# Causal attention: score chunks in pairs of PSUM banks with one exponential per pair, and the low parts of the probabilities multiplied side by side at a block's end

## The chip, the cores and the metric

The kernel runs on one core of a Trainium2 chip. The metric is the device time of one execution in microseconds (us), from the first to the last instruction, as the median of several runs. The engines are TensorE (PE, with its weight load PEld), VectorE (DVE), ScalarE (ACT), GpSimd (POOL) and SyncE (SP). PE writes its results to PSUM, which has eight banks of 512 f32 per partition.

## The reference

The reference is a small decoder trunk: one Mamba-2 layer, then one layer of multi-head latent attention, over 2048 tokens of 1024 channels. The change touches only the attention (16 heads, 96 channels for queries and keys, 64 for values):

```python
def causal_block_attention(q_nope, q_rope, k_nope, k_rope, v):
    scale = (QK_NOPE + QK_ROPE) ** -0.5
    for i in range(S // Q_BLOCK):
        q0 = i * Q_BLOCK
        kv_len = q0 + Q_BLOCK
        s = jnp.einsum('bqhd,bkhd->bhqk', q_nope[:, q0:kv_len], k_nope[:, :kv_len]) + \
            jnp.einsum('bqhr,bkr->bhqk', q_rope[:, q0:kv_len], k_rope[:, :kv_len])
        s = s.astype(jnp.float32) * scale
        mask = (q0 + local)[:, None] >= jnp.arange(kv_len)[None, :]
        p = jax.nn.softmax(jnp.where(mask, s, -jnp.inf), axis=-1).astype(v.dtype)
        outs.append(jnp.einsum('bhqk,bkhd->bqhd', p, v[:, :kv_len]))
```

## The kernel before, in words

The program has three stages, one after the other on PE: the Mamba layer and the projections for queries, keys and values (`layers`), the attention (`attention`, `heads`), and the gate, the output projection and the last norm (`back`). Numbers that need more than one pass of PE's precision are kept as a high and a low part.

**Blocks, rows, chunks.** For each of 16 heads there are four query blocks (0 to 3) of 512 queries. A block has four rows of 128 queries. A row's scores run over all keys up to its diagonal and are cut (`cuts`) into chunks of 256 to 512 keys: one chunk a row in block 0, two in block 1, three in block 2, four in block 3, 40 a head. What follows is per chunk, row or block:

- Scores, per chunk: three products of PE (L85 to L87: high by high, high by low, low by high) into one bank `mm` of PSUM. The row's last chunk also gets the causal mask added by a product (L1046, or L1044 in the first row). The pool gives out four banks `mm` in turn; another four, `tr`, serve transposes and outputs. The first 18 chunks of the stage take `tr` and `mm` in turn.
- Maximum: DVE takes the maximum of each chunk (L1047, `mx`). At a row's end it takes the maximum of those, negated (L1051, `nm`).
- Exponential, per chunk: ACT (L1059) reads the bank, subtracts `nm`, writes the probabilities `Pr` and sums them into `sm`; this frees the bank. DVE adds a row's sums (L1063).
- Transposes, "T", per 128 keys of a block: PE turns the four rows' probabilities (L1074) into one bank `tr`. ACT copies the bank to f16 as the high part (L116), DVE makes the low part from bank and high part (L117); both lie in one tile `PTs`.
- Value products, "V": PE multiplies the 128 columns of the values (64 high, 64 low) with the high part (L1084) and with the low part (L1085), 512 columns of queries or fewer at the diagonal. All go into one bank, the output `O`, whose partitions 0 to 63 and 64 to 127 are added by the store. After the block's last one, ACT copies the bank (L1091) and it is stored.

**Order.** PE's order in this stage is written by hand: `ahead` yields after every chunk, and the table `CREDIT` says for each chunk of a row which T and V follow it, from chunk 20 on (`LAG`). So the score chunks run some 20 chunks ahead of the T and V of their block. A V is taken once more than two T are held (`DEPTH`). The orders of DVE, ACT and POOL come from a scheduler at build time; every engine works through its queue in order. PE's next row can begin when a bank `mm` is free, that is when the exponential of the chunk four places before is done; that exponential needs its row's `nm`, and so the maximum of its row's last chunk.

Of the kernel before, what the change touches and what calls it, by code (L numbers as in the profile page):

```python
# [20 lines left out]
P = 128  # L21
# [47 lines left out]
class Net:  # L69
# [5 lines left out]
    def name(self, s):  # L75
        self.n += 1
        return f"{s}_{self.n}"

    def t(self, pool, tag, shape, dt=F32, bufs=None):
        return pool.tile(shape, dt, name=self.name(tag), tag=tag, bufs=bufs)  # L80


# [227 lines left out]
    def layers(self):  # L310
        with ExitStack() as ctx:
            tc = self.tc
            early = ExitStack()
# [682 lines left out]
    def attention(self):  # L996
        with ExitStack() as ctx:
            self.wo = self.tail.enter_context(self.tc.tile_pool(name="wo", bufs=1, side="right", reuse_waits="tile"))
            self.wraw = []
            sp = ctx.enter_context(self.tc.tile_pool(name="asp", bufs=2, reuse_waits="tile"))  # L1000
            with self.tc.manual_schedule(engines={mybir.EngineType.PE}):
                self.heads(sp)

    def heads(self, sp):
        nc, v = self.nc, self.nc.vector
        begun = []
# [12 lines left out]

        def scores(h, qb, st):  # L1020

            if h + 1 < NH:
                if qb == 2:
                    self.load_k(h + 1, 0, NB)
                    self.load_v(h + 1)
                self.load_q(h + 1, qb)
            Q, K = quer.pop((h, qb)), keys[h]
            late = []
            for j in range(4):
                qs = slice(j * P, (j + 1) * P)  # L1030
# [3 lines left out]
                banks = []  # L1034
                for n, (c0, w) in enumerate(parts):
                    if late:
                        late.pop(0)()
                    begun.append(0)
# [3 lines left out]
                    if n == nb - 1:  # L1042
                        if qb == j == 0:
                            nc.tensor.matmul(s[:, 0:w], self.idb, self.mk, start=False, stop=True)  # L1044
                        else:
                            nc.tensor.matmul(s[:, w - P:w], self.idb, self.mk[:, 0:P], start=False, stop=True)  # L1046
                    v.tensor_reduce(mx[:, n:n + 1], s[:, :w], AX.X, ALU.max)  # L1047
# [3 lines left out]
                v.tensor_reduce(nm, mx[:, :nb], AX.X, ALU.max, negate=True)  # L1051
                p = {}
                sm = self.t(sp, "sm", [P, 4], bufs=4)
                st["P"].append(p)

                def exp(n, j=j, nb=nb, parts=parts, banks=banks, nm=nm, p=p, sm=sm):
                    s, w = banks[n]
                    x = self.t(sp, "Pr", [P, TB], bufs=NP)
                    nc.scalar.activation(x[:, :w], s[:, :w], AF.Exp, bias=nm, accum_out=sm[:, n:n + 1])  # L1059
                    for c in range(0, w, P):  # L1060
                        p[(parts[n][0] + c) // P] = x[:, c:c + P]
                    if n == nb - 1:
                        v.tensor_reduce(sums[h][:, 4 * qb + j:4 * qb + j + 1], sm[:, :nb], AX.X, ALU.add)  # L1063

                late += [lambda n=n, f=exp: f(n) for n in range(nb)]
            for f in late:
                f()

        def turn(h, qb, kb, st):

            jj = max(kb - 4 * qb, 0)
            pt = self.t(self.pp, "tr", [P, TB], bufs=4)
            for j in range(jj, 4):
                nc.tensor.transpose(pt[:, j * P:(j + 1) * P], st["P"][j][kb], self.ident)  # L1074
# [3 lines left out]
            return u[:, :, c], c  # L1078

        def values(h, qb, kb, st, u, c):  # L1080
            if kb == 0:
                st["O"] = self.t(self.pp, "tr", [P, TB], bufs=4)
            nk = 4 * qb + 4
            nc.tensor.matmul(st["O"][:, c], vals[h][:, kb, :], u[:, 0], start=kb == 0, stop=False)  # L1084
            nc.tensor.matmul(st["O"][:, c], vals[h][:, kb, :], u[:, 1], start=False, stop=kb == nk - 1)  # L1085
            if kb == nk - 1:
                finish(h, qb, st)

        def finish(h, qb, st):
            o = self.t(sp, "Os", [P, TB], bufs=3)  # L1090
# [18 lines left out]
        states = [{"P": []} for _ in jobs]  # L1109
        sums = {}  # L1110
        def ahead():
            for n, (h, qb) in enumerate(jobs):
# [5 lines left out]
        held = []  # L1118

        def work(what):  # L1120

# [2 lines left out]
                held.append((a, turn(*a)))  # L1124
            elif what == "V" and held and (len(held) > DEPTH or not units):
                a, (u, c) = held.pop(0)
                values(*a, u, c)

        step = 0
        for credit in ahead():  # L1130
            step += 1
            if step > LAG:
                for what in credit:
                    work(what)
        while units or held:
            work("T")
            work("V")


    def back(self):  # L1140
        nc, a, v, hp = self.nc, self.a, self.nc.vector, self.hp
        with ExitStack() as ctx:
            sp = ctx.enter_context(self.tc.tile_pool(name="bsp", bufs=2, reuse_waits="tile"))
            self.sp = sp
            us = self.t(self.sm, "us", [P, KD])
            nc.sync.dma_start(us, self.us_d.rearrange("(k p) -> p k", p=P))
# [186 lines left out]
```

## Time and profile before

| what | value |
|---|---|
| median of 3 runs (lowest to highest) | 3209.99 us (3205.72 to 3210.55) |
| the profiled execution itself, its span | 3210.4 us, 3208.6 us |
| granted TensorE clock, mean | 0.997 |
| attention stage, from its first score product to its end | 2095 to 3027 us of the span |
| time of a head in the middle of that stage | 57 us |
| memory traffic | 322 MB read, 115 MB written, 136 GB/s |

A stretch of the profile gives for each engine its busy time and, in brackets, its instructions. A row of the timeline gives the start and the length in us, the engine, the line, the operation, out<-in by the program's names, and in square brackets the idle time before it and who ended it. A group gives the count, then the busy time in us and the mean length of one in ns. A matmul's length holds the depth of the array's pipeline: its pace is the distance from one start to the next. Lines are those of the kernel before; in the changed one L85 to L87 are L92 to L94, L1074 is L1090, L1084 is L1099, L1085 is L1110, L1059 is L1071 and L1047 is L1059.

### The profile page before, as it was taken

To read this page: it belongs to the slowest core of one execution; us is meant where nothing else is said; L and a number is where in the kernel's file an instruction comes from. 1 tells how busy PE (TensorE), PEld (TensorE's weight loads), DVE (VectorE), ACT (ScalarE), POOL (GpSimd) and SP (SyncE) were. 2 spreads that over 40 slices of the span, in tenths; PEclk is the share of its full clock that TensorE was granted. 3 is DMA by queue.
4 is the path that set the end of the run, shared out by engine and by line. 5 is a ranking of instruction groups with operands and counts; after the bars stand their busy time and mean duration, and the time that the engine had idled before them with its cause. 6 is when DMAs were issued, how large, how long until landed. Compare 5 with 4: busy or idle time off the path is not lost.

```text
span 3208.6 us, 52002 instructions
## 1 busy us (share of the span) xinstructions
PE 3101.7 (97%) x17735; PEld 2245.6 (70%) x17735; DVE 2511.8 (78%) x5330; ACT 2024.2 (63%) x5123; POOL 661.9 (21%) x895
## 2 busy tenths in 40 slices
PE   8999999999999999999999999999999999999998
PEld 6777654555655566555888888877777777777776
DVE  6888898888777787877876665678888888888665
ACT  7878566665555554556656554477877778778522
POOL 1222123322122212321121211322222122122100
PEclk9999999999999999999999999999999999999999
DMA  5333445553343344423376655853444444444485
GB/s 176 99 98 106 136 150 210 166 164 129 102 148 96 101 129 160 136 89 122 114 261 216 223 194 194 261 115 76 91 82 85 84 78 94 80 98 99 113 260 156
DMA packets 208632, 440.61 MB, mean 137 GB/s; under 512 B 28464, under 2 KB 62256, under 8 KB 206928
## 3 DMA queue, kind: packets, MB, share of 16 engines
q1 hardware_dynamic: 160672, 290.86, 29.4%
q0 software_dynamic: 47696, 146.44, 17.8%
q8 instruction: 140, 2.29, 0.3%
q14 instruction: 124, 1.02, 0.1%
HBM read 321.85 MB, written 115.35 MB: 136 GB/s over the span
## 4 chain that ended last, share of the span: by engine, by line
PE 62%; DVE 17%; ACT 7%; DMA 6%; issue 6%; POOL 1%; SPq 1%; ACTq 0%; DVEq 0%; POOLq 0%
PE mm L85 12%; PE mm L87 12%; PE mm L86 12%; PE tr L1074 6%; DVE cacc L488 4%; PE tr L86 3%; PE tr L1084 3%; PE tr L1085 3%; PE tr L85 3%; PE tr L87 3%; DMA wraw<-in_ssm_w_in_dram 2%; DMA big<-cumT 2%; DVE big L661 1%; DVE wsp L112 1%; DMA os<-ri_d 1%
## 5 line engine op out<-in xcount | busy, mean ns | idle before, releaser
L117 DVE SCALAR_TENSOR_TENSOR PTs<-tr,PTs 128x512 f16<-128x512 f32 (+3 forms) x640 | 374.4, 606 | 93.0 <-ACT PTs L116 87.3
L116 ACT ACTIVATE PTs<-tr 128x512 f16<-128x512 f32 (+3 forms) x640 | 328.1, 540 | 140.3 <-PE tr L1074 139.6
L1047 DVE TENSOR_REDUCE mx<-mm 128x1 f32<-128x512 f32 (+2 forms) x631 | 375.0, 606 | 45.4 <-PE mm L87 43.0
L1059 ACT ACTIVATE Pr<-mm,nm 128x512 f32<-128x512 f32 (+2 forms) x631 | 395.1, 635 | 22.9 <-DVE nm L1051 21.4
L1074 PE MATMUL tr<-pack,Pr 128*128 128x128 f32 x2176 | 317.5, 273 | 1.5 <-ACT Os L1091 1.4
L87 PE MATMUL mm<-xT,wsp 128*128 128x512 f16 (+1 forms) x800 | 308.3, 386 | 3.5 <-DVE wsp L117 2.3
L85 PE MATMUL mm<-xT,wsp 128*128 128x512 f16 (+1 forms) x800 | 311.4, 389 | 0.0
L85 PE MATMUL mm<-K,xT 96*128 96x512 f32 (+2 forms) x639 | 286.1, 448 | 23.3 <-ACT Pr L1059 22.1
L86 PE MATMUL mm<-xT,wsp 128*128 128x512 f16 (+1 forms) x800 | 308.1, 385 | 0.0
L1074 PEld LDWEIGHTS tr<-pack,Pr 128*128 128x128 f32 x2176 | 253.2, 141 | 50.0 <-ACT Os L1091 2.2
L675 ACT ACTIVATE Xw<-tr,d_wend 128x64 f32<-128x64 f32 x512 | 182.5, 357 | 93.5 <-DVE Xd L671 85.7
L85 PE MATMUL mm<-wsp,xT 128*128 128x512 f16 (+2 forms) x640 | 235.4, 368 | 4.5 <-ACT craw L482 4.4
L86 PE MATMUL mm<-wsp,xT 128*128 128x512 f16 (+2 forms) x640 | 234.0, 366 | 0.0
L87 PE MATMUL mm<-wsp,xT 128*128 128x512 f16 (+2 forms) x640 | 233.6, 366 | 0.0
L86 PE MATMUL mm<-K,xT 96*128 96x512 f32 (+2 forms) x639 | 231.2, 362 | 0.0
L87 PE MATMUL mm<-K,xT 96*128 96x512 f32 (+2 forms) x639 | 231.0, 361 | 0.0
L488 DVE SCALAR_TENSOR_TENSOR cacc<-craw,pack,cacc 128x512 f32<-128x512 f32 x288 | 217.1, 776 | 10.3 <-ACT cacc L486 9.3
L1084 PE MATMUL tr<-PTs,xT 128*128 128x512 f16 (+3 forms) x640 | 222.0, 348 | 0.1
L1085 PE MATMUL tr<-PTs,xT 128*128 128x512 f16 (+3 forms) x640 | 219.4, 347 | 0.0
L85 PE MATMUL mm<-wsp,yT 128*128 128x512 f32 x512 | 208.5, 408 | 3.3 <-DVE hs L545 2.1
L633 POOL TENSOR_TENSOR Xp<-Xw,Xp 128x512 fp32r<-128x512 f32 x64 | 83.0, 1296 | 607.7 <-ACT Xp L632 395.0
L87 PE MATMUL mm<-wsp,yT 128*128 128x512 f32 x512 | 204.3, 399 | 0.0
(420 smaller groups left out, 7818.9 us busy)
## 6 DMA issues: line engine op xcount, KB each, us to landing
wraw<-in_ssm_w_in_dram SPq DMA_DIRECT2D x128, 256.0 KB, 3.0
big<-cumT SPq DMA_DIRECT2D x64, 512.0 KB, 4.8
wraw<-in_ssm_w_out_dram SPq DMA_DIRECT2D x128, 256.0 KB, 2.7
wsp<-w_d SPq DMA_DIRECT2D x64, 512.0 KB, 3.7
w_d<-wsp POOLq DMA_DIRECT2D x32, 512.0 KB, 4.5
xT<-qn_d POOLq DMA_DIRECT2D x64, 256.0 KB, 4.6
K<-kn_d POOLq DMA_DIRECT2D x15, 1024.0 KB, 8.2
wraw<-in_mla_w_uq_dram SPq DMA_DIRECT2D x36, 256.0 KB, 4.9
```

Source lines behind the costliest of these rows:

```text
L85: mm(out, l_hi, r_hi, start=start, stop=False)
L86: mm(out, l_hi, r_lo, start=False, stop=False)
L87: mm(out, l_lo, r_hi, start=False, stop=stop)
L116: self.nc.scalar.activation(hi, src, AF.Copy, scale=scale)
L117: self.nc.vector.scalar_tensor_tensor(lo, src, scale, hi, ALU.mult, ALU.subtract)
L488: nc.vector.scalar_tensor_tensor(acc, raw[:, k:k + TB], wk[k], acc, ALU.mult, ALU.add)
L675: act(Xw[:, hc], px[:, hc], AF.Copy, scale=wend[:, h0 + h:h0 + h + 1])
L1047: v.tensor_reduce(mx[:, n:n + 1], s[:, :w], AX.X, ALU.max)
L1059: nc.scalar.activation(x[:, :w], s[:, :w], AF.Exp, bias=nm, accum_out=sm[:, n:n + 1])
L1074: nc.tensor.transpose(pt[:, j * P:(j + 1) * P], st["P"][j][kb], self.ident)
L1084: nc.tensor.matmul(st["O"][:, c], vals[h][:, kb, :], u[:, 0], start=kb == 0, stop=False)
L1085: nc.tensor.matmul(st["O"][:, c], vals[h][:, kb, :], u[:, 1], start=False, stop=kb == nk - 1)
```

## The change

- The scores of two neighbouring chunks go to one tile `pair` of two banks; two such tiles take the place of the four banks `mm`. `cuts` gives pairs of equal widths (or a single chunk), so some rows have 2 x 320, 2 x 384 or 2 x 448 in place of 512 and a rest. The count of chunks and of maxima stays. The first 18 chunks no longer use `tr`.
- One exponential serves a pair: 24 a head in place of 40, up to 1024 wide. A row with one exponential (blocks 0 and 1) has its sum copied by POOL in place of added by DVE.
- High and low part of the transposed probabilities are two tiles, 5 and 18 of them. `values` multiplies only the high part. The low parts are kept until the block's last V; then `lows` multiplies them with the 64 high columns of the values alone, the even ones into partitions 0 to 63 of `O`, the odd ones into 64 to 127. The product of the low values with the low probabilities is left out. `lows` runs at the end of the next row of scores, or ahead of the next block's first V. Only then is `O` copied and stored.
- `CREDIT`, `LAG` and `DEPTH` are unchanged.

```diff
-NP = 24
+NP = 14
+NL = 18
...
+        self.pm = ctx.enter_context(self.tc.tile_pool(name="pm", bufs=4, space=PSUM, reuse_waits="tile"))
...
             while at < kv:
-                w = min(TB, kv - at)
-                if kv - at == TB + P:
-                    w = 384
-                out.append((at, max(w, 256)))
+                w = min(2 * TB, kv - at)
+                if kv - at == 2 * TB + P:
+                    w -= P
+                out.append((at, 1, max(w, 256)) if w <= TB else (at, 2, w // 2))
                 at += w
...
-                    s = self.t(self.pp, "tr" if len(begun) <= 18 and len(begun) % 2 == 1 else "mm", [P, TB], bufs=4)
-                    ks = slice(c0, c0 + w)
-                    self.mm3(s[:, :w], Q[:, 0, qs], Q[:, 1, qs], K[:, 0, ks], K[:, 1, ks], True, n < nb - 1)
...
-                    v.tensor_reduce(mx[:, n:n + 1], s[:, :w], AX.X, ALU.max)
-                    banks.append((s, w))
-                    yield CREDIT[qb][j][n]
+                for c0, m, w in parts:
+                    for i in range(m):
+                        if late:
+                            late.pop(0)()
+                        if i == 0:
+                            pair = self.t(self.pm, "pair", [P, 2, TB], bufs=2)
+                            banks.append(pair[:, :m, :w])
+                        s, ks = pair[:, i, :w], slice(c0 + i * w, c0 + i * w + w)
+                        end = n == total - 1
+                        self.mm3(s, Q[:, 0, qs], Q[:, 1, qs], K[:, 0, ks], K[:, 1, ks], True, not end)
...
+                        v.tensor_reduce(mx[:, n:n + 1], s, AX.X, ALU.max)
+                        yield CREDIT[qb][j][n], end
+                        n += 1
...
-                    x = self.t(sp, "Pr", [P, TB], bufs=NP)
-                    nc.scalar.activation(x[:, :w], s[:, :w], AF.Exp, bias=nm, accum_out=sm[:, n:n + 1])
+                    x = self.t(sp, "Pr", [P, 2 * TB], bufs=NP)[:, :m * w]
+                    nc.scalar.activation(x.rearrange("p (m w) -> p m w", m=m), banks[n], AF.Exp, bias=nm,
+                                         accum_out=sm[:, n:n + 1])
...
-            u = self.t(sp, "PTs", [P, 2, TB], F16, bufs=5)
-            self.pair16(u[:, 0, c], u[:, 1, c], pt[:, c], PSCALE)
+            hi, lo = self.t(sp, "PTh", [P, TB], F16, bufs=5), self.t(sp, "PTl", [P, TB], F16, bufs=NL)
+            self.pair16(hi[:, c], lo[:, c], pt[:, c], PSCALE)
...
-            nc.tensor.matmul(st["O"][:, c], vals[h][:, kb, :], u[:, 0], start=kb == 0, stop=False)
-            nc.tensor.matmul(st["O"][:, c], vals[h][:, kb, :], u[:, 1], start=False, stop=kb == nk - 1)
+            nc.tensor.matmul(st["O"][:, c], vals[h][:, kb, :], u[0], start=kb == 0, stop=False)
...
+        def lows(h, qb, st):
+            nk = len(st["lo"])
+            for i, (kb, l, c) in enumerate(st["lo"]):
+                d = slice(i % 2 * 64, i % 2 * 64 + 64)
+                nc.tensor.matmul(st["O"][d, c], vals[h][:, kb, 0:64], l, start=False, stop=i >= nk - 2)
+            finish(h, qb, st)
...
             if step > LAG:
+                if end and owed:
+                    lows(*owed.pop())
```

On PE, the last two chunks of row 1 of block 3 in a middle head stood as follows (`mm` are score banks, K the keys, xT the queries, mk and idb the mask; in brackets the engine whose semaphore a row waits for):

```order
L85 MATMUL mm_24712<-K_23572,xT_23810 128x512 [waits Activation_49]
L86 MATMUL mm_24712<-K_23572,xT_23810 128x512
L87 MATMUL mm_24712<-K_23572,xT_23810 128x512
L85 MATMUL mm_24720<-K_23572,xT_23810 128x256 [waits Activation_49]
L86 MATMUL mm_24720<-K_23572,xT_23810 128x256
L87 MATMUL mm_24720<-K_23572,xT_23810 128x256
```

In the changed program the same two chunks on PE are halves of one tile `pair`:

```order
L92 MATMUL pair_24674<-K_23538,xT_23780 128x384 [waits Activation_49]
L93 MATMUL pair_24674<-K_23538,xT_23780 128x384
L94 MATMUL pair_24674<-K_23538,xT_23780 128x384
L92 MATMUL pair_24674<-K_23538,xT_23780 128x384 [waits DVE_49]
L93 MATMUL pair_24674<-K_23538,xT_23780 128x384
L94 MATMUL pair_24674<-K_23538,xT_23780 128x384
```

The widths became equal, and the second chunk waits for DVE: in the program the awaited count is that of the maximum over the first chunk of the same tile. All 256 pairs with two chunks have this wait.

On ACT, around the change from row 1 to row 2 of that block, before (`PTs` are high copies of transposes, `Pr` exponentials):

```order
L116 ACTIVATE PTs_24698<-tr_24694 128x384 [waits PE_49,Activation_49]
L116 ACTIVATE PTs_24731<-tr_24728 128x256 [waits PE_49,Activation_49]
L116 ACTIVATE PTs_24736<-tr_24734 128x128 [waits PE_49,Activation_49]
L1059 ACTIVATE Pr_24755,sm_24753<-mm_24689,nm_24751 128x512 [waits DVE_49]
L116 ACTIVATE PTs_24746<-tr_24741 128x512 [waits PE_49,Activation_49]
L1059 ACTIVATE Pr_24770,sm_24753<-mm_24703,nm_24751 128x512
```

On ACT, at the same place in the changed program:

```order
L123 ACTIVATE PTh_24662<-tr_24658 128x384 [waits PE_49,Activation_49]
L123 ACTIVATE PTh_24688<-tr_24685 128x256 [waits PE_49,Activation_49]
L123 ACTIVATE PTh_24694<-tr_24692 128x128 [waits DVE_49,PE_49]
L1071 ACTIVATE Pr_24713,sm_24711<-pair_24653,nm_24709 128x1024 [waits DVE_49]
L123 ACTIVATE PTh_24704<-tr_24699 128x512 [waits PE_49,Activation_49]
L1071 ACTIVATE Pr_24729,sm_24711<-pair_24674,nm_24709 128x768
```

The copies keep their places ahead of the first exponential, and that one now reads 1024 columns; the next row's first chunk waits for it.

On PE, where query block 1 (eight units of T and V) ends, the changed program has its low parts in one batch (`tr_24635` is the output, 64 partitions wide in each row):

```order
L1110 MATMUL tr_24635<-PTl_24643,xT_23541 64x512
L1110 LDWEIGHTS xT_23541
L1110 MATMUL tr_24635<-PTl_24663,xT_23541 64x384
L1110 LDWEIGHTS xT_23541
L1110 MATMUL tr_24635<-PTl_24689,xT_23541 64x256
L1110 LDWEIGHTS xT_23541
L1110 MATMUL tr_24635<-PTl_24695,xT_23541 64x128
L1090 MATMUL tr_24760<-pack,Pr_24391 128x128
```

Before, each of these stood right behind its high product (L1084, then L1085, both 128 partitions); now the last four of eight stand in a row behind a row of scores, and the transposes follow.

More of the change, by code (lines that the diff above doesn't have):

```diff
@@ L312, in layers @@
             tc = self.tc
+            self.banks(ctx)
             early = ExitStack()
@@ L999, in attention @@
             self.wraw = []
+            self.banks(ctx)
             sp = ctx.enter_context(self.tc.tile_pool(name="asp", bufs=2, reuse_waits="tile"))
@@ L1033, in scores @@
                 mx = self.t(sp, "mx", [P, 4], bufs=4)
[L1034 to L1038, printed above, removed]
[L1039 to L1049 removed]
+                banks, n = [], 0
+                total = sum(m for _, m, _ in parts)
+                for c0, m, w in parts:
[8 more added lines that the diff above has]
+                        self.mm3(s, Q[:, 0, qs], Q[:, 1, qs], K[:, 0, ks], K[:, 1, ks], True, not end)
+                        if end:
+                            if qb == j == 0:
+                                nc.tensor.matmul(s, self.idb, self.mk, start=False, stop=True)
+                            else:
+                                nc.tensor.matmul(s[:, w - P:w], self.idb, self.mk[:, 0:P], start=False, stop=True)
+                        v.tensor_reduce(mx[:, n:n + 1], s, AX.X, ALU.max)
+                        yield CREDIT[qb][j][n], end
+                        n += 1
                 nm = self.t(sp, "nm", [P, 1], bufs=4)
[L1051 removed]
+                v.tensor_reduce(nm, mx[:, :total], AX.X, ALU.max, negate=True)
                 p = {}
@@ L1126, in work @@
                 a, (u, c) = held.pop(0)
+                if a[2] == 0 and owed:
+                    lows(*owed.pop())
                 values(*a, u, c)
         step = 0
-        for credit in ahead():
+        for credit, end in ahead():
             step += 1
             if step > LAG:
+                if end and owed:
+                    lows(*owed.pop())
                 for what in credit:
@@ L1143, in back @@
             sp = ctx.enter_context(self.tc.tile_pool(name="bsp", bufs=2, reuse_waits="tile"))
+            self.banks(ctx)
             self.sp = sp
```

28 lines of the change are left out of this document (17 added, 11 removed).

## The prediction

> **What bounds the kernel now.** I read the page's engine line first, then the attention stage alone, then its waits, then single rows. The engine line and the chain that ended last say that TensorE (PE) carries the kernel:
>
> ```profile
> span 3208.6 us, 52002 instructions
> PE 3101.7 (97%) x17735; PEld 2245.6 (70%) x17735; DVE 2511.8 (78%) x5330; ACT 2024.2 (63%) x5123; POOL 661.9 (21%) x895
> PE 62%; DVE 17%; ACT 7%; DMA 6%; issue 6%; POOL 1%; SPq 1%; ACTq 0%; DVEq 0%; POOLq 0%
> ```
>
> The change touches the attention, so the stretches of that stage matter (columns: length; busy time of PE, weight load, DVE, ACT, POOL; clock):
>
> ```profile
> 2095.00:3027.00 932.00, 906.26 (x5696) 693.34 (x5694) 773.23 (x1833) 733.83 (x2012) 202.64 (x297) 1.00 0.43 86
> 2227.00:2284.00 57.00, 55.73 (x355) 42.81 (x354) 48.01 (x115) 45.19 (x128) 12.02 (x20) 1.00 0.42 84
> 2455.00:2512.00 57.00, 55.73 (x355) 42.81 (x354) 48.00 (x115) 45.20 (x128) 12.02 (x20) 1.00 0.43 84
> ```
>
> The reader sees a strict period: one head every 57.00 us, sixteen heads in 932 us, PE idle 1.27 us a head. DVE and ACT have 9 and 12 us to spare, so PE's own stream sets the pace, as long as no wait is put into it. The waits of that stage show how little PE stands still:
>
> ```profile
> DVE mx L1047 <- PE mm L87: 43.0, 82, 1.9
> PE mm L85 <- ACT Pr L1059: 22.1, 22, 1.9
> ```
>
> PE waits for one thing only, the exponential that frees a score bank: 22 times, so about once a head. One such place, in query block 3 between rows 0 and 1 of a middle head:
>
> ```profile
> 2406.21 0.69 ACT L1059 ACTIVATE Pr<-mm,nm 128x512 f32<-128x512 f32 x1
> 2407.04 0.50 PE L85 MATMUL mm<-K,xT 96*128 96x512 f32 x1 [1.21 <-ACT Pr L1059]
> 2407.38 0.40 PE L86 MATMUL mm<-K,xT 96*128 96x512 f32 x1
> 2407.62 0.40 PE L87 MATMUL mm<-K,xT 96*128 96x512 f32 x1
> 2407.85 0.50 PE L1074 MATMUL tr<-pack,Pr 128*128 128x128 f32 x3
> 2408.05 0.69 DVE L1047 TENSOR_REDUCE mx<-mm 128x1 f32<-128x512 f32 x1 [1.23 <-PE mm L87]
> ```
>
> From it: a score product streams 0.24 us (2407.38 to 2407.62); a maximum begins 0.20 us after the chunk's stream has ended (2407.85 to 2408.05) and takes 0.69; PE starts 0.14 us after ACT's end (2406.90 to 2407.04), and its first product then takes 0.34 in place of 0.24, 0.10 more.
>
> **Gain: low parts side by side.** Per head now 28, 4, 4 and 4 low products of four widths (13 heads in these rows):
>
> ```profile
> L1085 PE MATMUL tr<-PTs,xT 128*128 128x512 f16 x364 | 137.9, 379 | 0.0
> L1085 PE MATMUL tr<-PTs,xT 128*128 128x384 f16 x51 | 16.6, 326 | 0.0
> L1085 PE MATMUL tr<-PTs,xT 128*128 128x256 f16 x51 | 13.9, 272 | 0.0
> L1085 PE MATMUL tr<-PTs,xT 128*128 128x128 f16 x51 | 11.2, 219 | 0.0
> 2410.47 0.38 PE L1084 MATMUL tr<-PTs,xT 128*128 128x512 f16 x1
> 2410.68 0.38 PE L1085 MATMUL tr<-PTs,xT 128*128 128x512 f16 x1
> ```
>
> The means count the pipeline's depth; the pace is start to start, 0.21 us for 512 columns, and by width 0.16, 0.11 and 0.055. That is 28 x 0.21 + 4 x 0.325 = 7.2 us a head. In pairs (12 of 512 with 512, and per block one of 512 with 384 and one of 256 with 128): 12 x 0.21 + 4 x 0.32 = 3.8. Saved: **3.4 us a head**, if halves of the array do run together. The scan already does this (L683: one output on two partition halves):
>
> ```profile
> 500.70 0.39 PE L653 MATMUL tr<-BC,BC 128*128 128x128 f32 x2
> 500.92 0.38 PE L85 MATMUL mm<-xT,wsp 128*128 128x512 f16 x1
> 508.91 0.38 PE L87 MATMUL mm<-xT,wsp 128*128 128x512 f16 x1
> 509.22 1.15 PE L683 MATMUL tr<-Xd,big 128*64 128x64 f32 x32
> 510.30 0.50 PE L85 MATMUL tr<-Sp,Ct 128*128 128x512 f32 x1
> ```
>
> A 128-column pass of plain f32 takes 0.11 us (two in 0.22), so 64 columns alone would take 0.055; 32 of them in 1.08 us are 0.034 each. So they overlap. On both sides of that group some 0.1 us is lost (508.91 + 0.21 to 509.22). Four batches a head with two sides each: **0.8 us lost**, bounds 0 and 1.6. [...]
>
> **Cost: the second half of a pair waits for the first half's maximum.** A pair is one tile. In the built program the second chunk of each of the 256 two-bank pairs waits for DVE, at the count of the maximum over the first chunk of the same pair; before, each chunk had a tile of its own. Behind it on PE stand the row's other chunks, transposes and value products, and DVE and ACT live on those. After the first chunk's stream that is 0.20 + 0.69 + 0.14 + 0.10 = 1.13 us for 512 columns; for 384 the maximum is shorter, 1.00 in all, and between and below these widths I go by the line: 1.06 for 448, 0.93 for 320.
>
> ```profile
> L1047 DVE TENSOR_REDUCE mx<-mm 128x1 f32<-128x512 f32 x325 | 220.9, 684 | 35.3 <-PE mm L87 34.0
> L1047 DVE TENSOR_REDUCE mx<-mm 128x1 f32<-128x384 f32 x90 | 49.2, 547 | 0.2 <-PE mm L87 0.2
> 2411.66 0.60 PE L1074 MATMUL tr<-pack,Pr 128*128 128x128 f32 x4
> 2412.10 0.33 PE L1084 MATMUL tr<-PTs,xT 128*128 128x384 f16 x1
> ```
>
> What PE has between the two chunks covers it: four transposes 0.44, a value product 0.21. By the order of work that is: block 1, nothing, four times (4.1 us); block 2, 0.88, 0.65, 0.32, 0.39 (2.2 us left); block 3, first pairs, 0.44, 0.33, 0.44, 0.65 (2.7 us), second pairs nothing but one 0.055 (4.1 us). Sum **13 us a head**; without the 0.24 of hop and refill it would be 9, with twice that 17. To this comes DVE's queue: in the eight rows of blocks 2 and 3 low copies (L117, as long as a maximum) of the row before stand ahead of the first maximum. Bounds 0 and 8 x 0.69 = 5.5; I take the middle, **3**.
>
> **Cost: a row begins on the pair that the row before still holds.** Four banks held four chunks; now they hold two pairs. In blocks 2 and 3 a row needs both, so its first chunk waits for the row before: its last chunk, maximum, row maximum, then an exponential twice as wide. ACT starts that one only after the high copies (L116) that stand ahead of it:
>
> ```profile
> 2386.65 0.23 PE L1046 MATMUL mm<-mk,idb 128*128 128x128 bf16 x1
> 2388.77 0.69 ACT L1059 ACTIVATE Pr<-mm,nm 128x512 f32<-128x512 f32 x1
> 2410.40 0.23 PE L1046 MATMUL mm<-mk,idb 128*128 128x128 bf16 x1
> 2411.82 0.69 ACT L1059 ACTIVATE Pr<-mm,nm 128x512 f32<-128x512 f32 x1
> L1059 ACT ACTIVATE Pr<-mm,nm 128x512 f32<-128x512 f32 x324 | 222.1, 694 | 13.8 <-DVE nm L1051 12.5
> L1059 ACT ACTIVATE Pr<-mm,nm 128x256 f32<-128x256 f32 x104 | 51.7, 497 | 0.0
> ```
>
> From the end of the mask product (0.06 of stream) to the exponential it is 2.05 us in block 2 and 1.35 in block 3. A 1024-wide one takes 0.69 + 512 x (694 - 497) / 256 ns = 1.08; no row shows it: bounds 0.69 and 2 x 0.69, I take the line through the two widths shown. With 0.14 and 0.10 the row starts 2.6 to 3.3 us after the mask; PE's cover there shrinks with the value products. Block 2, row 0: copies come 0.43 earlier, 2.05 - 0.43 + 0.99 (896 wide) + 0.24 - 1.08 of cover = 1.8. Rows 1 and 2 likewise 1.8 each; row 3 is covered by sixteen low products (1.8). Block 3, row 1: 1.35 + 1.08 + 0.24 - 1.36 = 1.3; by the same sum the others there are 1.2, 0.8 (a transpose waits for a bank that the held output keeps) and 0.7, and the next block 0's second row 1.0. Sum 10.4, of which 1.2 is there now: **9.2 us a head**, 6 to 12 by the bounds of the wide exponential.
>
> **Edits at nothing.** 256 fewer exponentials and their sums free ACT, and 128 reductions go from DVE to POOL: both have slack in the 57 us row, and rather help the bounds above. Buffer counts (14 wide probabilities, 18 low copies) block no PE row that isn't counted. Before the attention every engine's order is the same. Without the transposes' banks the first 18 chunks run on two pairs: 0 to 12 us once, I take 5.
>
> **Sum.** 57.0 - 3.4 + 0.8 + 13 + 3 + 9.2 = 79.6 us a head, 22.6 more; x 16 = 362, + 5 = 367. On the profiled execution's 3210.4 us (0.4 from the median shown) that is 3577; I say **3570 us**.
>
> **Rivals.**
> 1. Only the row starts cost (the second halves find their maximum done): 57 - 2.6 + 9.2, 6.6 x 16 = 106, 3316 us. For it: DVE idles 9 us a head. Against: in eleven of sixteen pairs under 0.4 us of work stands between the halves, and the maximum of 384 or 512 alone is 0.55 to 0.68.
> 2. Not slower: the waits hide behind transposes and the low batches, and the packing's 2.6 us and the 1.2 of today's wait come free: 3.8 x 16 = 61, 3149 us. It decides if all new waits stay under 3.8 us a head; the rows give 26.
> 3. The halves of the array don't overlap: 3.4 x 16 = 54 more, 3624 us. L683 speaks against it.
> 4. The clock falls. PE would stand still some 26 of 80 us. In the scan a gap does this:
>
> ```profile
> 410.15 1.04 PE L87 MATMUL mm<-xT,wsp 128*128 128x512 f16 x4 [2.32 <-DVE wsp L117]
> 411.40:414.80 3.40, 3.40 (x10) 1.18 (x8) 3.40 (x7) 3.39 (x12) 1.52 (x2) 0.50 0.94 325
> ```
>
> 2.32 us of idling, then 3.4 us at clock 0.50, which costs half of them, 1.7. My longest wait is 1.8 us; if a window fell every second row, 8 x 1.7 x 16 = 218 more, 3788 us. [...]
>
> **How the numbers follow.** Forecast 0.74, rival 1 0.08, rival 2 0.04, rival 3 0.06, rival 4 0.06, no change 0.02. With second halves at 9 to 16 us a head, row starts at 6 to 12, the queue at 0 to 5 and the switches at 0 to 1.6, a head takes 11.6 to 31.2 us more, and the time runs from about 3390 to 3720; rival 3 lies inside, so 0.80 does. Faster by over 0.2% (about what a measurement of this kernel can tell from none) 0.04, within 0.02, slower 0.94.
>
> **What would show it.** Right: the period near 80 us; PE's score rows waiting for DVE's maximum some 250 times, about 1 us each, and for the exponential some 8 times a head; low products in pairs a few ns apart, each pair 0.21 us on. Wrong: no row of PE waiting for DVE; a period under 65; clock rows at 0.50 in the attention; an exponential of 1024 far from 1.1 us.

## The result, and the profile after

The changed kernel takes 3663.7 us (median of 4 runs, 3660.59 to 3674.48); measured beside it the kernel before takes 3209.4. The ratio is 1.1414, with a 95% interval of 1.1399 to 1.1430: slower by 14%. The profiled execution took 3661.3 us. (One execution of an experiment further down took 6606 us, with PE busy in 6536 of them where it is busy in 3102 before, for as many products; it is left out, and that kernel was traced again.)

The first two lines of the page, and of the stretches the whole attention and one head of it (length; busy time of PE, weight load, DVE, ACT, POOL; clock):

```profile
span 3659.5 us, 51484 instructions
PE 3273.0 (89%) x17735; PEld 2282.6 (62%) x17735; DVE 2533.2 (69%) x5202; ACT 1977.0 (54%) x4611; POOL 684.6 (19%) x1023
2100.00:3478.00 1378.00, 1073.48 (x5696) 727.95 (x5696) 792.67 (x1703) 682.80 (x1498) 226.04 (x424) 0.91 0.26 58
2449.30:2534.40 85.10, 66.79 (x353) 45.27 (x353) 49.19 (x106) 42.13 (x93) 13.54 (x27) 0.90 0.26 56
```

The attention grew from 932 to 1378 us, which is nearly all of the change; a head takes 81 to 86 us in place of 57.00. DVE and ACT do what they did, and PE is busy only 67 of 85 us. The last column but two is what the prediction did not have: a granted clock of 0.91. The waits of PE in the stage (in total, times, longest):

```profile
PE pair L92 <- DVE mx L1059: 160.6, 214, 1.5
PE pair L92 <- ACT Pr L1071: 117.3, 112, 2.0
PE tr L1090 <- ACT Os L1115: 8.3, 16, 0.5
```

Both new waits stand there. A second half in block 3, in the timeline:

```profile
2511.51 0.58 PE L92 MATMUL pair<-K,xT 96*128 96x512 f32 x1
2511.93 0.40 PE L93 MATMUL pair<-K,xT 96*128 96x512 f32 x1
2512.16 0.40 PE L94 MATMUL pair<-K,xT 96*128 96x512 f32 x1
2513.34 0.56 PE L92 MATMUL pair<-K,xT 96*128 96x512 f32 x1 [0.78 <-DVE mx L1059]
2513.70 0.63 PE L93 MATMUL pair<-K,xT 96*128 96x512 f32 x1
2514.13 0.63 PE L94 MATMUL pair<-K,xT 96*128 96x512 f32 x1
```

The first half's stream ends 0.24 us after 2512.16; the second begins at 2513.34, 0.94 later (1.03 was worked out, and 0.10 for the refill). The last two rows are longer, 0.63 in place of 0.40, and 0.43 apart in place of 0.24: just ahead of them, at 2513.63, the clock fell. Two neighbouring stretches of 3.41 us, the second from the moment at which it fell:

```profile
2510.22:2513.63 3.41, 2.19 (x8) 1.37 (x9) 2.48 (x5) 0.31 (x1) 0.82 (x1) 1.00 0.28 38
2513.63:2517.04 3.41, 3.41 (x14) 2.50 (x14) 1.42 (x3) 1.20 (x2) 1.98 (x4) 0.50 0.13 35
```

PE stood idle 1.22 of the first 3.41 us, in two gaps of under 0.8 (the first began ahead of this stretch), and the next 3.41 us ran at 0.50. In the attention the clock falls 35 times, for 3.41 to 34 us each, 256 us together, with PE busy in 232 of them; at half pace that loses at most 116 us. In the attention of the kernel before it never falls. The longest fall stands at the stage's start. From the first score product to the first transpose, before and then changed:

```profile
2094.80:2109.50 14.70, 13.76 (x75) 10.49 (x74) 12.42 (x40) 11.17 (x36) 8.52 (x15) 1.00 0.99 214
2100.00:2136.80 36.80, 25.91 (x75) 16.83 (x76) 13.15 (x32) 9.87 (x24) 9.52 (x22) 0.55 0.31 79
```

The same 20 chunks take 22 us longer there, 12 of them with PE busy at the lower clock and 10 with PE idle. The low products in a batch, and what follows it:

```profile
2504.78 0.23 PE L1058 MATMUL pair<-mk,idb 128*128 128x128 bf16 x1
2504.95 0.94 PE L1110 MATMUL tr<-PTl,xT 128*64 128x512 f16 x8
2505.82 0.66 PE L1090 MATMUL tr<-pack,Pr 128*128 128x128 f32 x4
2505.90 1.11 ACT L1071 ACTIVATE Pr<-pair,nm 128x1024 f32<-128x1024 f32 x1 [3.97 <-DVE nm L1063]
L1071 ACT ACTIVATE Pr<-pair,nm 128x1024 f32<-128x1024 f32 x144 | 161.2, 1119 | 130.3 <-DVE nm L1063 130.3
```

Eight products (four pairs) take 0.87 us of PE, from the batch's start to the next product's, some 0.1 of it for the batch's sides; inside, two halves start 3 ns apart and a pair of 512 takes 0.213. The halves of the array do run together. The exponential of 1024 takes 1.12 us, where 1.08 was worked out.

For a comparison over several kernels I take PE's starts in eleven middle heads: the distance to the next start, less what that form takes in an unbroken stream (0.231 us for a score product of 512, 0.215 for a value product of 512, 0.109 for a transpose), put down to what the next instruction waited for. "Packed" and "pairs" are the two parts of the change alone, of the experiments below.

| us a head | before | changed | packed | pairs |
|---|---|---|---|---|
| period | 57.0 | 84.3 | 61.4 | 78.5 |
| PE's stream, unbroken, full clock | 54.5 | 50.8 | 50.8 | 54.5 |
| starts delayed by a wait | 1.6 | 22.9 | 6.4 | 20.0 |
| sides of the packed batches | 0 | 1.1 | 1.0 | 0 |
| half clock, at most (half of PE's busy time at 0.50 in these heads) | 0 | 6.6 | 0.8 | 0.9 |
| rest (not assigned; refills behind waits are in it) | 0.9 | 2.9 | 2.4 | 3.1 |

### The profile page after: what moved, and what is told of

Read it like the earlier page. It is cut to its first block, busy times and chain, and to the rows that moved or that the text cites. A ratio compares the mean times of both kernels' runs of the same rounds, so it can differ in the third digit from the quotient of the medians.

```text
span 3659.5 us, 51484 instructions
## 1 busy us (share of the span) xinstructions
PE 3273.0 (89%) x17735; PEld 2282.6 (62%) x17735; DVE 2533.2 (69%) x5202; ACT 1977.0 (54%) x4611; POOL 684.6 (19%) x1023
## 3 DMA queue, kind: packets, MB, share of 16 engines
q1 hardware_dynamic: 160672, 290.86, 25.2%
q0 software_dynamic: 47696, 146.44, 14.7%
## 4 chain that ended last, share of the span: by engine, by line
PE 51%; DVE 23%; ACT 12%; issue 7%; DMA 6%; POOL 1%; SPq 0%; ACTq 0%; DVEq 0%; POOLq 0%
PE mm L92 7%; PE mm L94 7%; PE mm L93 7%; PE pair L92 5%; DVE mx L1059 5%; DVE PTl L124 4%; ACT PTh L123 4%; PE tr L1090 3%; ACT Pr L1071 3%; PE pair L94 3%; DVE cacc L496 3%; PE pair L93 3%; PE tr L93 3%; PE tr L92 3%; PE tr L94 3%
## 5 line engine op out<-in xcount | busy, mean ns | idle before, releaser
L1059 DVE TENSOR_REDUCE mx<-pair 128x1 f32<-128x512 f32 (+4 forms) x640 | 387.1, 611 | 294.5 <-PE pair L1058 152.4
L92 PE MATMUL pair<-K,xT 96*128 96x512 f32 (+4 forms) x640 | 320.2, 500 | 289.9 <-DVE mx L1059 160.6
L123 ACT ACTIVATE PTh<-tr 128x512 f16<-128x512 f32 (+3 forms) x640 | 323.2, 536 | 450.0 <-PE tr L1090 449.0
L124 DVE SCALAR_TENSOR_TENSOR PTl<-tr,PTh 128x512 f16<-128x512 f32 (+3 forms) x640 | 371.8, 607 | 224.8 <-ACT PTh L123 220.1
L1071 ACT ACTIVATE Pr<-pair,nm 128x1024 f32<-128x1024 f32 (+6 forms) x384 | 334.8, 875 | 216.5 <-DVE nm L1063 172.9
L92 PEld LDWEIGHTS pair<-K,xT 96*128 96x128 f32 x640 | 130.2, 203 | 437.5 <-DVE mx L1059 242.1
L1090 PE MATMUL tr<-pack,Pr 128*128 128x128 f32 x2176 | 353.8, 293 | 15.6 <-ACT Os L1115 8.3
L1090 PEld LDWEIGHTS tr<-pack,Pr 128*128 128x128 f32 x2176 | 277.4, 152 | 71.4 <-issue 15.6
L93 PE MATMUL pair<-K,xT 96*128 96x512 f32 (+4 forms) x640 | 252.2, 394 | 0.0
L94 PE MATMUL pair<-K,xT 96*128 96x512 f32 (+4 forms) x640 | 252.1, 394 | 0.0
L1099 PE MATMUL tr<-PTh,xT 128*128 128x512 f16 (+3 forms) x640 | 215.7, 365 | 0.0
L92 PE MATMUL mm<-wsp,yT 128*128 128x512 f32 x512 | 209.1, 410 | 3.1 <-DVE hs L553 1.8
L93 PE MATMUL mm<-wsp,yT 128*128 128x512 f32 x512 | 204.7, 400 | 0.0
L94 PE MATMUL mm<-wsp,yT 128*128 128x512 f32 x512 | 204.6, 400 | 0.0
```

The costliest lines, as they stand in the source:

```text
L92: mm(out, l_hi, r_hi, start=start, stop=False)
L93: mm(out, l_hi, r_lo, start=False, stop=False)
L94: mm(out, l_lo, r_hi, start=False, stop=stop)
L123: self.nc.scalar.activation(hi, src, AF.Copy, scale=scale)
L124: self.nc.vector.scalar_tensor_tensor(lo, src, scale, hi, ALU.mult, ALU.subtract)
L1059: v.tensor_reduce(mx[:, n:n + 1], s, AX.X, ALU.max)
```

## The experiments

The theory was the prediction's: the packing gains PE time, and the pairs cost by two separate waits. The rivals: the waits are one chain, so that one taken away comes back at another place; the clock, not the waits, makes part of the loss; and the time that the packing saves PE is not time of the kernel.

**The packing alone.** The score part is that of the kernel before, the low parts that of the change:

```diff
-pair = self.t(self.pm, "pair", [P, 2, TB], bufs=2)
+s = self.t(self.pp, "tr" if len(begun) <= 18 and len(begun) % 2 == 1 else "mm", [P, TB], bufs=4)
```

> The scores as before (single banks, an exponential for each), the low parts in packed batches as in the change. If the batches gain what the prediction says (3.4 us a head, 0.8 of it lost at their sides), the period is 54.4 us and the time 3209 - 2.6 x 16 = 3168 us. If the batch brings a stall of its own (the output is kept longer, its bank missing for transposes), the time is 3209 or above. If the halves of the array do not overlap, the products take their old 7.2 us a head and the switches come on top: 3209 + 0.8 x 16 = 3222.

It took 3282.9 us, 1.0215 times the kernel before (1.0198 to 1.0233): 70 us slower, where 42 faster was expected. The trace comes from a second run (3281.2 us):

> The kernel with only the packed batches once more, for its trace, since the profiled execution of the first run had PE at half its pace throughout. 3283 us, a period of some 61.6 us. If the loss comes of the batch's place (all low products of a block in one of its rows), PE waits little in the row with the batch, and in the other rows stands still for exponentials and transposes' banks some 8 us a head in all. If it comes of the products themselves, a pair takes far over 0.21 us, or the switches at the sides far over 0.1 us each.

Its attention, and the wait of PE that is largest in total there; before it was 22.1 us, 22 times:

```profile
2097.00:3100.00 1003.00, 920.09 (x5698) 672.73 (x5696) 771.38 (x1833) 737.10 (x2012) 203.69 (x297) 0.99 0.40 80
PE mm L92 <- ACT Pr L1069: 69.0, 71, 3.5
```

The products themselves do as expected: PE's stream falls by 3.7 us a head and the batches' sides cost 1.0. But starts delayed by a wait go from 1.6 to 6.4. The saving was real for PE and came back as waiting, for the exponential above all, with the sides on top.

**The pairs alone.** The changed kernel, each low product behind its high one again:

```diff
-            nc.tensor.matmul(st["O"][:, c], vals[h][:, kb, :], u[0], start=kb == 0, stop=False)
-            st["lo"].append((kb, u[1], c))
+            nc.tensor.matmul(st["O"][:, c], vals[h][:, kb, :], u[:, 0], start=kb == 0, stop=False)
+            nc.tensor.matmul(st["O"][:, c], vals[h][:, kb, :], u[:, 1], start=False, stop=kb == nk - 1)
```

> The scores in pairs as in the change, each low product behind its high one as before. If the two parts of the change simply add, this is the changed kernel's 3664 plus the 2.6 us a head that the packing saves, about 3705 us. If the low products fill waits of PE that stand there anyway (they lie between the chunks, where PE waits for maximum or exponential), they are partly free: 3620 to 3665, and the packing then gains nothing beside the pairs.

3573.0 us, 1.1123 times before (1.1103 to 1.1143). Below both expectations: the packing does not merely gain nothing beside the pairs, it costs 91 us there. The stage and the waits of this kernel:

```profile
2098.00:3389.00 1291.00, 1032.64 (x5696) 709.73 (x5694) 804.33 (x1704) 683.52 (x1498) 226.38 (x424) 0.97 0.29 62
PE pair L92 <- DVE mx L1059: 136.2, 223, 1.3
PE pair L92 <- ACT Pr L1071: 109.2, 112, 2.0
```

The waits are there without the packing, about 20 us a head. With it they are 2.9 longer, the sides are 1.1, and that eats the 3.7 saved. What is left of the 91 us goes with the clock: 0.97 here, 0.91 with the packing, 82 us at half clock against 256, worth at most 81 us.

**Second halves without their wait.** The changed kernel, the first half's maximum taken behind the second half's products:

```diff
-v.tensor_reduce(mx[:, n:n + 1], s, AX.X, ALU.max)
+if i == m - 1:
+    for o in range(m):
+        v.tensor_reduce(mx[:, n - i + o:n - i + o + 1], pair[:, o, :w], AX.X, ALU.max)
```

> The changed kernel with one edit: the maximum over a pair's first chunk is taken after the products of its second chunk, ahead of that one's maximum, so that no second chunk waits for DVE. If the second halves cost 13 us a head and the queue ahead of them 3, as predicted, most of that goes; the last maximum of a row comes up to 0.69 us later, for eight rows a head some 5 us; and with fewer gaps the clock falls less. Then the period is some 66 to 70 us, and the time 3360 to 3430. If the waits are one chain (what PE no longer waits at a second half it waits at the next row's start, since the same exponential frees the pair), the time stays within 3600 to 3680.

3647.7 us, 1.1371 (1.1316 to 1.1425): 16 us under the changed kernel, which the two intervals do not tell apart.

```profile
2095.00:3454.00 1359.00, 1072.47 (x5696) 778.90 (x5694) 769.93 (x1704) 704.00 (x1498) 227.13 (x424) 0.86 0.27 58
PE pair L92 <- ACT Pr L1073: 273.3, 135, 3.1
```

No second half waits for DVE any more, and PE waits for the exponential 273 us in place of 117. Of the 161 us taken away 156 stand there. That fits the rival (one chain), but does not show it, because the edit itself lengthens the way to a row's start: the first half's maximum now comes behind the second half, in front of the row's last ones on DVE. In the rows of blocks 2 and 3 (eleven middle heads) the row's maximum `nm` begins on average 2.66 us after the mask product in place of 1.05, and the next row's first chunk 4.56 after it in place of 3.16; for 128 rows that is some 180 us, more than the 156. The clock also drops to 0.86 (389 us at half clock, PE busy in 369, at most 185 lost against 116). Without that difference the edit would be worth up to 85 us, 5 a head.

**Work into the gaps.** The changed kernel with products of zeros ahead of the second halves:

```diff
+def fill(n):
+    if n > 0 and live and live[0][1]:
+        for _ in range(n):
+            nc.tensor.matmul(live[0][0], zero[:, 0:P], zero, start=False, stop=False)
...
+                fill(gap - sum(2 if what == "T" else 1 for what in credit))
```

> The changed kernel with up to five products of zeros (512 columns, 0.21 us each) into the open output ahead of each second chunk, fewer where transposes or value products stand there: 855 products, some 180 us of work that adds nothing to the result, at places where PE waits 160 us in the trace. If the half-clock windows (35 of them, 256 us of the attention at 0.50) come from the share of idle time and cost up to 128 us, the idle share falls, most windows go, and the time falls by 40 to 100 us, to 3560 to 3620, with more work on PE. If the clock costs nothing, since PE waits anyway, or if the windows come of something else, the time stays at 3664 or rises by up to 60 us.

3609.4 us, 1.1238 (1.1218 to 1.1258): 54 us faster than the changed kernel, with 855 products more.

```profile
2096.00:3427.00 1331.00, 1153.92 (x6551) 753.29 (x6551) 793.25 (x1706) 679.82 (x1498) 227.08 (x424) 0.97 0.28 60
PE pair L92 <- ACT Pr L1080: 129.4, 127, 2.0
PE pair L92 <- DVE mx L1068: 26.9, 81, 1.3
```

PE's wait for the maximum fell from 160.6 to 26.9 us, the time at half clock from 256 to 85. The wait for the exponential did not shrink (129 us, 117 before), so what the zeros bring back is the clock's, and it had come of PE's idling: more work took less time.

**Batches of four.** The packed kernel with single banks, a batch behind each fourth value product:

```diff
-            if kb == 4 * qb + 3:
-                owed.append((h, qb, st))
+            if kb % 4 == 3:
+                lows(h, qb, st, kb == 4 * qb + 3)
```

> As the kernel with only the packed batches, but a batch of four low products (two pairs) behind each fourth value product, in place of one batch a block. The pairs gain the same 3.4 us a head, and ten batches in place of four lose at most 10 x 0.2 = 2.0 at their sides. If the loss of the block-wide batches is one of place, this is faster than before: 57.0 - 3.4 + 2.0 = 55.6 us a head or somewhat less, 3165 to 3195 us. If column halves and switches cost more than they gain, more switches are worse still: 3283 or above.

3258.8 us, 1.0147 (1.0130 to 1.0164). Better than one batch a block, and still slower than before. By PE's starts the ten batches' sides cost 2.8 us a head, and the waits are 4.3, 2.7 more than before: the 3.7 saved are more than gone.

**Low products one behind the other.** The packed kernel with nearly all in one half of the array:

```diff
-                d = slice(i % 2 * 64, i % 2 * 64 + 64)
+                d = slice(64, 128) if i == nk - 1 else slice(0, 64)
```

> As the kernel with only the packed batches (3283 us), but all low products go to partitions 0 to 63 except each block's last, so that they run one behind the other: 7.0 us of PE a head in place of 3.8. If PE's time in the batch is exposed (nothing else waits longer than it), the time rises by 3.2 x 16 = 51, to 3334. If the batch stands where PE would wait anyway, it stays at 3283. If the halves do not overlap in truth, it stays at 3283 too, but then the trace of the kernel above shows pairs of 0.42 us.

3328.1 us, 1.0366 (1.0349 to 1.0384): 45 us more than packed, of the 51 of PE's extra work. A batch of block 3 in this kernel, and then in the packed one:

```profile
2497.89 3.27 PE L1104 MATMUL tr<-PTl,xT 128*64 128x512 f16 x16
```

```profile
2544.41 1.81 PE L1104 MATMUL tr<-PTl,xT 128*64 128x512 f16 x16
```

The batch's length lies bare: nine tenths of what it grows by is time of the kernel. So packing shortens a batch as promised; it is putting the low products into a batch that costs.

**Filler where the low products stood.** The packed kernel, a product of zeros behind each high value product:

```diff
+            nc.tensor.matmul(st["O"][:, c], vals[h][:, kb, :], zero[:, c], start=False, stop=False)
```

> The kernel with only the packed batches (3283 us), with a product of zeros as long as the high one behind each high value product, where the low product stood before: 7.2 us more of PE a head that add nothing to the result. If the packing lost because the shorter value products no longer cover the way to a row's first bank (PE waits 6.4 us a head there, 1.6 before the change), the filler stands in those waits: the time stays within 3270 to 3310, of which 57.0 + 3.8 + 1.0 = 61.8 us a head (3286) is the sum of PE's work alone. If PE's work bounds that kernel and the loss is of another kind, the filler costs all of its 7.2 x 16 = 115 us: 3380 to 3400.

3272.4 us, 1.0189 (1.0169 to 1.0209): some 115 us more of PE's work, and no more time (10 us less, which the two intervals do not tell apart; the packed kernel loses up to 12 us at half clock).

```profile
2101.00:3094.00 993.00, 987.02 (x6336) 728.92 (x6335) 777.42 (x1834) 732.18 (x2011) 202.93 (x297) 1.00 0.40 81
PE mm L92 <- ACT Pr L1072: 3.0, 5, 1.0
```

PE is busy 987 of 993 us and waits 3. A low product behind its high one costs the packed kernel nothing, since PE has to wait there. That is why shortening it gained nothing.

**The batch as cover.** Batches at a row's end, ahead of the next row's first chunk; then also all transposes and value products of a row behind its last chunk:

```diff
+                if end and owed:
+                    h, qb, st = owed[0]
+                    n = len(st["lo"])
+                    if st["n"] == 4 * qb + 4 or n >= 4:
+                        lows(*owed.pop())
...
-    (("T", "", "", "VVTTVTV"), ("T", "V", "", "VTTVTV"), ("T", "V", "V", "TVTTV"), ("TV", "V", "", "TVTVT")),
+    (("", "", "", "TVTVTVTV"), ("", "", "", "TVTVTVTV"), ("", "", "", "TVTVTVTV"), ("", "", "", "TVTVTVTV")),
```

> Single banks and packed low products, in batches of four (now and then two or six) at the end of a row, just ahead of the next row's first chunk. PE's own work is then some 51 us a head and ten batches at up to 0.4 us for their sides, 55. If the waits for the exponential at the rows' starts are what eats the gain, the batch of 0.85 us and its sides now cover most of them: a period of 55 to 57.5, 3175 to 3220 us. If the waits come of something that the place of the batch doesn't touch (the vector engine's queue as a whole), it stays near the batches behind each fourth value product: 3245 to 3270.

> As the kernel before it in this list, and the order of work by hand changed for rows of blocks 2 and 3: all transposes and value products behind the row's last chunk (in block 2 all but one transpose), in turn, so that the last maximum finds a shorter queue on the vector engine and the cover ahead of a row's start is as long as it can be. If cover and queue at the row's start are all that PE waits for, a period of 54.5 to 56.5 us, 3170 to 3205. If four transposes in a row run into their three free banks, PE waits for low copies in place of exponentials, and the time is that of the kernel before it or above, 3210 to 3280.

3278.4 us, 1.0211 (1.0190 to 1.0232), and 3272.7, 1.0188 (1.0169 to 1.0207). The place of the batch alone does not help. In the first PE waits 56 us for exponentials, in the second 36, and 17 for low copies that transposes' banks wait for. My theory that cover at the row starts would bring the gain back fell here.

**The exponential first.** Once on the kernel with pairs alone, once (with a fixed order) on the packed kernel: a row's maximum and its exponentials, or its first one, ahead of the copies of transposes.

```diff
-                        yield CREDIT[qb][j][n], end
+                        if not end:
+                            yield CREDIT[qb][j][n], end
...
+                for n in range(nb):
+                    exp(n)
+                yield CREDIT[qb][j][total - 1], True
```

```diff
+                yield CREDIT[qb][j][nb - 1], (top, exp(0))
...
+                    for one in end or ():
+                        behind.enter_context(self.tc.issue_after(one.ins))
```

> The kernel with pairs alone (3573 us) with one edit: a row's maximum and exponentials are written ahead of the transposes and value products of its last chunk, not behind them, so that on ACT two or three high copies no longer stand ahead of a wide exponential, nor low copies ahead of the row's maximum on DVE. PE's order is unchanged. If the pairs' loss is one chain through two slots (products, maxima, row maximum, exponential, next row's products), shortening it by 0.7 to 1.4 us for some eight rows a head gains 90 to 180 us: 3390 to 3480. If each second half's own wait is what costs, as the prediction's separate terms have it, only the row starts get cheaper, by at most the 109 us that PE waits for exponentials in that kernel, and the second halves stay: 3460 to 3530. If the high copies now come late for PE, it rises.

> The kernel with only the packed batches (3283 us) with one edit in the order of the other engines: a row's own maximum and its first exponential are held ahead of the copies of the transposes that stand behind its last chunk on PE; before, one to three low copies stood ahead of the row's maximum in 109 of 256 rows. PE's order is unchanged. If the gain of the packing is lost in the way from a row's last chunk to its first exponential (PE waits 6.4 us a head), taking up to 0.7 us from some seven such ways a head leaves 1 to 2 us of waits and no half-clock windows: 56 to 58 us a head, 3190 to 3225 us, about the kernel before or under it. If ACT and DVE are short of time as a whole in these rows, so that any order of their work makes PE wait as long, transposes wait for copies in place of chunks for exponentials, and the time stays at 3260 to 3300.

Both lost, the second by more than either of its ranges allows: 3615.5 us, 1.1259 (1.1242 to 1.1275), 43 above the pairs alone, and 3335.4 us, 1.0370 (1.0343 to 1.0397), 53 above packed. PE's waits in the first, then in the second:

```profile
PE pair L92 <- DVE mx L1059: 131.4, 175, 1.7
PE pair L92 <- ACT Pr L1072: 89.6, 90, 2.0
PE tr L1091 <- DVE PTs L124: 33.6, 41, 1.0
```

```profile
PE tr L1087 <- DVE PTl L124: 90.2, 93, 2.3
PE mm L92 <- ACT Pr L1070: 25.7, 68, 1.0
```

In the packed kernel the wait for exponentials falls from 69 to 26 us, and transposes wait 90 us for low copies in place of 7. Shortening one way lengthens the other: ACT and DVE carry both the scores' way to a free bank and the transposes' way to a free bank, and whichever stands behind makes PE wait. In the kernel with pairs the clock did much of the rest (157 us at half clock, 82 without the edit, up to 34 us).

## Why the prediction was right, and where it was not

The time, 3664 us, lies in the range of 3390 to 3720, 94 above the 3570 named, and the two waits that were to make it so are in the trace. The terms did not all come out, and errors offset each other.

1. **Second halves wait for the maximum: right.** 214 waits with DVE's maximum behind them, 0.75 us each by the wait's length, and some 0.16 more from the end of the stream (0.94 against 0.78 in the row above); about 250 were predicted, at about 1 us.
2. **Row starts wait for the wide exponential: right.** 112 times, seven a head where eight were predicted, 1.05 us each. In block 2 they are 1.4 to 1.6 us where 1.8 was named, with none behind the row that a long batch covers, as predicted; in block 3 they are 0 to 0.7 where 0.7 to 1.3 was named.
3. **Their sum: a little too large.** Predicted 25.2 us a head for both (13 + 3 + 9.2). The table's delayed starts grew by 21.3, in the pairs alone by 18.4, refills aside. Whether they may be added as separate terms stays open: with the second halves' wait gone, as much appeared at the row starts, but that edit also put the row's maximum 1.6 us later.
4. **"3.4 us a head" saved by the packing, 0.8 lost at its sides: right for PE (3.7 and 1.0), wrong for the kernel.** The step that fails is "PE's own stream sets the pace". In the kernel before PE idled only 1.27 us a head, but with shorter value products PE waits instead, 4.8 us a head more in the packed kernel, and the batch stands in the open. The runs with filler and with low products one behind the other add up to this: nothing is gained where the low products stood, and the batch is paid nearly in full. With its 4.8 us (3.8 of products, 1.0 of sides) a head would take 57.0 + 4.8 = 61.8, and the packed kernel takes 61.4. That fits a way over DVE and ACT that was about as long as PE's own work; no run measures that way by itself. Alone the packing costs 4.4 us a head in place of gaining 2.6. Rival 2, which rested on its gain, had nothing to stand on.
5. **The clock: wrong.** The forecast held it at full, as "my longest wait is 1.8 us", under the 2.32 us of the gap in the scan. The waits for a score bank were 2.0 us at most, hardly longer, and it fell all the same, which costs at most 116 us, 7.3 a head. Rival 4 had the right effect with 0.06 of the chance, at 13.6 us a head: it priced single gaps, where the falls went with the idle time summed over 3.41 us (last section). The zeros brought 54 us of the loss back.
6. **Lead-in 5 us: much too small.** The stage's start takes 22 us more, where 12 was the upper bound: 36.8 us in place of 14.7, by the rows above. The pairs alone take 36.8 too, the packed kernel 14.7. The term had waits on two pairs in it, and no clock.

So the time lies in the range, in part by luck. A head took 84.3 us in place of 79.6: the waits came out 3.9 smaller, the clock took up to 6.6 and the rest grew by 2.0; with the 17 us that the lead-in took beyond its 5, that is about the 94 us. That the head's errors partly cancel was not foreseen. Rival 3 (no overlap) is refuted by the pairs of 0.213 us, and by the 45 us more of the kernel that has them one behind the other.

What stays open is what exactly holds the packed kernels at 60 to 61 us a head when their PE work is some 52 to 54. The runs show that it is not PE's work, that a longer batch adds to it nearly in full, and that changing the order on ACT and DVE moves the wait and does not remove it. That the batch starves ACT and DVE of transposes is argued from the timeline, not tested by itself. The 3.97 us of ACT quoted above began 3 us ahead of that batch; in the packed kernel DVE is 72 to 99% busy while a batch runs, and idles 0.5 to 1.95 us behind it, ahead of its next low copy. No version here beats the kernel before.

## What to carry to other kernels

An engine that is 98% busy (PE here, 55.73 of 57.00 us a head) need not be the only bound: in the packed kernel 3.7 us a head less of its work brought 4.8 us more of its waiting, by my reading because the way over the other engines is about as long. The test is cheap: filler in the place of what was cut, some 115 us of it, cost nothing here. Two chunks in one tile are one thing to the program: the second waits for the reader of the first (214 waits, 160.6 us, in the changed kernel), and the tile is free only when the last reader is done. Before adding waits to a full TensorE, price the clock by the idle time in a stretch of 3.41 us, not by the longest gap: in the changed kernel 1.17 us of it was the least ahead of a fall to 0.50.

## What the runs showed of the hardware

- The falls of the granted clock went with idle time summed over a stretch, more than with its longest gap. The falls of one execution lie on one grid of 3.41 us, to within 3 ns. I laid that grid over the whole execution in the changed kernel and three experiments (pairs alone, second halves without their wait, work into the gaps). Of the some 90 stretches at full clock with PE idle 1.9 us or more, all but three or four were followed by half clock; with 0.9 us or less, none of over 3400; between them some (in the changed kernel 28 of 131, from 1.17 us on). Single gaps were often short: the two above are 0.77 and 0.78 us, and 15 of the 42 falls of the changed kernel stand behind stretches with no longer gap than that.
- Once at half, the clock came back mostly after a stretch with almost no idle time: of the stretches at half clock with 0.5 us of idle time or more in the changed kernel, none of 20 was followed by full clock; of the 63 with less, 42 were.
- A batch on halves of the array costs 0.09 to 0.12 us as it begins and 0.15 to 0.19 as it ends, by PE's starts (packed kernel and batches of four), where 0.1 a side was read from the scan.
